# A relative-position bias table moved from the kernel's start to a place between two projection tiles

## The chip, the cores and the metric

One core of a Trainium2 chip runs the whole kernel. The metric is the device time of one execution in microseconds; several executions are timed, and their median counts. All data are float32.

## What is computed

One decoder layer is applied to a prompt group (1 x 1024 tokens) and a sample group (8 x 8 tokens, with key and value caches of 2048 rows) by the same weights: RMSNorm with adaLN shift and scale, one input projection `h @ w_in` to queries, keys, values and a pooling input, attention in three dilated windows, causal pooling, an output projection, and a channel sub-layer of width 4096. What matters here is the bias of the attention. Each branch adds, by head, a bias that depends on the distance between query and key alone:

```python
bias = rel_bias[rel_bucket(jnp.clip(dist, 0, n_sub) * dil)]
logits = logits + jnp.transpose(bias, (2, 0, 1)).astype(jnp.float32)
logits = jnp.where(valid[None, :, None, None], logits, NEG_INF)
...
o, lse over the branches (128, 1), (512, 4), (2048, 16), merged by their softmax denominators
```

The kernel merges the three branches into one softmax. For each of the 8 heads it needs a table over distance: `rel_bias` of the bucket of a distance plus the log of the number of branches that hold that distance (or -1e30 where none does).

## The kernel before

**The order of the work.** The kernel is written in program order and a planner orders the instructions of each engine: an instruction comes when its inputs and buffers are there by the planner's own times, the earlier one in the program first. Buffers come in kinds ("tags") with a fixed number each: "nat" 17 (rows of all 1088 tokens), "raw" 4 (weights as loaded), "wf" 6 (weights split), "tmp" 2, and in PSUM "ps" 8 banks. `tc.issue_after(ins)` keeps the instructions of a block behind `ins` on its engine. On the chip each engine and each DMA queue then runs its list in that order and waits where it must. DMAs issued by `nc.sync` go through SP's queue, those issued by `G.dma_start` through GpSimd's.

**Start (lines 68 to 236).** SP loads the constants `cpk`, eight tiles `x` of 128 x 1088, then the bias tables (below), then the ada weights `wa` (eight tiles of 512 KB for one half, L93 to L97), `us`, and the first two projection weights win4 and win5. ScalarE squares the x tiles into `xsq` (x0 into `acc`), VectorE adds them to `acc` (L195), TensorE sums `acc` over partitions (L205, names `n1`), VectorE and ScalarE make the inverse root `rstd1` of it by a logarithm, an exponential and three Newton ops per half (`newton`, L132 to L135, 512 and 576 wide). Meanwhile TensorE multiplies the ada weights (L101, `pa`); the result is transposed (L110) and added to its bias (L115).

**The bias tables (L175 to L184, L217 to L228, L301 to L312).** `rel_bias` (32 x 8) and the table `onehot` (32 buckets x 3752 distances) come through SP's queue, the latter in four pieces of 1024 columns (`oh`); `logmult` comes as four pieces of 8 rows into `lm`, at partitions 0, 32, 64 and 96. TensorE multiplies each piece in two halves of 512 columns (L224, `pg`, all with `rbias` on partitions 0 to 31), ScalarE copies the eight results to `fb` (L228), and GpSimd adds `fb` to `lm` (L302). Then a copy that needs the last projection input (`mark`, L304) holds back five DMAs from GpSimd's queue: `lm` is written to DRAM, 16 times over, as `gscr` (L309), and its far part as `fscr` (L312). From there the attention reads its bias tiles: `bs` and `bnew` on GpSimd's queue (L386 to L394), `fs` on SP's (`load_bias`, L461).

**Projection inputs and tiles (L258 to L376).** `h1_half` makes, for four x tiles at a time, `hp` on VectorE (L264), its rounded part `h1h` on ScalarE (L265) and the rest `h1l` on VectorE (L279). `gemm` multiplies split weights with split inputs in three passes (L243, L245, L247) into three banks of PSUM per tile. The weights are split by ScalarE (L146) and by VectorE, or for win4 and win5 by GpSimd (L147). Key tiles are 4 to 7, query tiles 0 to 3. `in_tile` also runs two or three steps of the later ada products behind each tile. `QK.tile` copies a result to `nat` (L339) and squares it (L340); `stats` (L351 to L353) and `scale` (L361 to L363, names `kss`, `krb`, `krst`, `qrb`) normalise the keys:

```python
kg, qg = QK(4, gk, "k"), QK(0, gq, "q")
for r in range(4):
    kg.tile(r)
kg.stats()
qg.tile(0)
kg.scale()
```

Behind these stages follow the pooling and value tiles, the attention (an order written out by hand), the output projection and the channel sub-layer.

Of the kernel before, what the change touches and what calls it, by code (L numbers as in the profile page):

```python
# [11 lines left out]
F32 = mybir.dt.float32  # L12
# [5 lines left out]
P = 128  # L18
D = 1024
KD = D // P  # L20
# [5 lines left out]
H = 8  # L26
# [12 lines left out]
GLEN = 2312  # L39
FLEN = 15 * 96  # L40
GREP = 16
# [4 lines left out]
CTX = 15  # L46
# [3 lines left out]
def body(ctx: ExitStack, tc: tile.TileContext, i, o):  # L50
    nc = tc.nc
    mm = nc.tensor.matmul
    V = nc.vector
    S = nc.scalar
    G = nc.gpsimd

    def f(ap):
        return ap.bitcast(F32)

    const = ctx.enter_context(tc.tile_pool(name="const", bufs=1))  # L60
    pools = {"": tc.alloc_tile_pool(name="psum1", bufs=8, space=PSUM)}
    wpool = ctx.enter_context(tc.tile_pool(name="wpool", bufs=3))

    def ps(name, tag="ps"):
        return pools[""].tile([P, 512], F32, tag=tag, name=name, bufs=PSB[tag])
# [5 lines left out]
    def part(name):  # L71
        c0, shape = CPK[name]
        n = math.prod(shape)
        v = cpk[:, c0:c0 + n]
        if len(shape) == 2:
            v = v.rearrange("p (a b) -> p a b", b=shape[1])
        return v

    cT, bT, g1T, g2T, qkg, ident, ones, sel, selb, pscT, rcnt = (part(n) for n in CPK)
    gq = const.tile([P, 1], F32, tag="gq", name="gq")  # L80
    V.tensor_scalar_mul(gq, qkg[:, 0:1], E ** -0.5)
    gk = qkg[:, 1:2]
# [10 lines left out]
    def ada_load(r, hf, k, pool, tag, bufs):  # L93
        t = pool.tile([P, 2, 512], F32, tag=tag, name=f"wa{r}_{hf}_{k}", bufs=bufs)
        src = i["w_ada"][k * P:(k + 1) * P, r * 2048:(r + 1) * 2048].rearrange("p (s c) -> p s c", s=2)
        nc.sync.dma_start(t, src[:, :, hf * 512:(hf + 1) * 512])
        return t  # L97

    def ada_mm(pa, k, t):
        for g in range(4):  # L100
            ins = mm(pa[32 * g:32 * g + 32, :256], cs[:, k, :], t[:, g // 2, (g % 2) * 256:(g % 2 + 1) * 256],  # L101
                     start=(k == 0), stop=(k == KD - 1))
        return ins

    def ada_end(r, hf, pa):
        sb = (wpool if r else nat_pool).tile([P, 256], F32, tag="tmp" if r else "nat", name=f"adas{r}_{hf}", bufs=2 if r else NNAT)
        act = S.copy(sb, pa[:, :256])
        pt = ps(f"pat{r}_{hf}")
        for j in range(2):
            nc.tensor.transpose(pt[:, j * P:(j + 1) * P], sb[:, j * P:(j + 1) * P], ident)  # L110
        for j in range(2):
            src = pt[:, j * P:(j + 1) * P].rearrange("p (s q c) -> p s q c", s=2, c=32)[:, :, :, 0:9]
            idx = aT[:, r * 16:(r + 1) * 16, :].rearrange("p (s h q j) c -> p s h q j c", s=2, h=2, q=2)
            bb = bT[:, r * 16:(r + 1) * 16].rearrange("p (s h q j) -> p s h q j", s=2, h=2, q=2)[:, :, hf, :, j]
            V.tensor_tensor(idx[:, :, hf, :, j, :], src, bb.unsqueeze(3).to_broadcast([P, 2, 2, 9]), ALU.add)  # L115
        return act
# [43 lines left out]
    nat_pool = tc.alloc_tile_pool(name="nat", bufs=NNAT, side="left")  # L160
# [11 lines left out]

    gscr = tc.dram_tile([H, GREP, GLEN], F32, name="gscr")
    fscr = tc.dram_tile([H, FLEN], F32, name="fscr")
    rbias = const.tile([32, H], F32, tag="rbias", name="rbias")  # L175
    nc.sync.dma_start(rbias, i["rel_bias"])
    lm = nat_pool.tile([P, 1024], F32, tag="nat", name="lm")
    G0 = [(32 * n, c0, min(1024, GLEN + FLEN - c0)) for n, c0 in enumerate(range(0, GLEN + FLEN, 1024))]
    ohs = []
    for r0, c0, n in G0:  # L180
        oh = wpool.tile([32, 1024], F32, tag="wf", name=f"oh{c0}", bufs=NWF)
        nc.sync.dma_start(oh[:, :n], i["onehot"][:, c0:c0 + n])
        nc.sync.dma_start(lm[r0:r0 + H, :n], i["logmult"][:, c0:c0 + n])
        ohs.append(oh)  # L184
    wa0 = {(0, k): ada_load(0, 0, k, *(((wpool, "raw", NRAW), (nat_pool, "nat", NNAT))[k // 4])) for k in range(KD)}

    xs = nat_pool.tile([P, KD, NB, TS], F32, tag="nat", name="xs")
# [1 line left out]
    for k in range(KD):  # L189
        if k == 0:  # L190
            S.activation(acc, xts[0], AF.Square)
        else:
            sq = wpool.tile([P, T], F32, tag="tmp", name=f"xsq{k}", bufs=2)
            act = S.activation(sq, xts[k], AF.Square)
# [3 lines left out]
    def rstd_of(acc, rstd, chunks, name):  # L198

        a0, a1 = chunks[0][0], chunks[-1][0] + chunks[-1][1]  # L200
        vv = wpool.tile([P, T], F32, tag="tmp", name=f"{name}v", bufs=2)
        tv = wpool.tile([P, T], F32, tag="tmp", name=f"{name}t", bufs=2)
        for ci, (c0, n) in enumerate(chunks):
            pp = ps(f"{name}_{ci}")
            ins = mm(pp[:, :n], ones, acc[:, c0:c0 + n], start=True, stop=True)  # L205
            V.tensor_scalar(vv[:, c0:c0 + n], pp[:, :n], 1.0 / D, EPS, ALU.mult, ALU.add)
        half = [slice(a0, a0 + 512), slice(a0 + 512, a1)] if a1 - a0 > 600 else [slice(a0, a1)]
        for c in half:
            ln = S.activation(tv[:, c], vv[:, c], AF.Ln)
        with tc.issue_after(ln.ins):  # L210
            for c in half:
                S.activation(rstd[:, c], tv[:, c], AF.Exp, scale=-0.5)
        for c in half:
            newton(rstd[:, c], vv[:, c], tv[:, c])
        return ins

    fb = wpool.tile([P, 1024], F32, tag="wf", name="fb", bufs=NWF)  # L217
    pgs = []
    for d0 in (0, 512):
        pg = ps(f"pg{d0}")  # L220
        for (r0, c0, n), oh in zip(G0, ohs):
            if n > d0:
                w = min(512, n - d0)
                pe = mm(pg[r0:r0 + H, :w], rbias, oh[:, d0:d0 + w], start=True, stop=True)  # L224
                pgs.append((pg, slice(r0, r0 + H), d0, w))
    with tc.issue_after(act.ins):
        for pg, r, d0, w in pgs:
            S.copy(fb[r, d0:d0 + w], pg[r, :w])  # L228
    pa = ps("pa0_0")
    with tc.issue_after(pe.ins):  # L230
        pe = ada_mm(pa, 0, wa0[0, 0])
    with tc.issue_after(pe.ins):
        pe = rstd_of(acc, rstd1, CHUNKS, "n1")
    with tc.issue_after(pe.ins):
        for k in range(1, KD):
            pe = ada_mm(pa, k, wa0[0, k])
# [16 lines left out]
    h1h, h1l = [], []  # L253
# [35 lines left out]
    act = ada_end(0, 0, pa)  # L289
# [3 lines left out]
    pa = ps("pa0_1")  # L293
# [4 lines left out]
            ada_mm(pa, k, wa0[1, k])  # L298
    ada_end(0, 1, pa)
    h1_half(1)  # L300
    for r0, c0, n in G0:  # L301
        G.tensor_add(lm[r0:r0 + H, :n], lm[r0:r0 + H, :n], fb[r0:r0 + H, :n])  # L302
    mark = const.tile([P, 1], F32, tag="mark", name="mark")
    ins = G.tensor_copy(mark, f(h1l[KD - 1][:, 0:1]))  # L304
    with tc.issue_after(ins.ins):
        for r0, c0, n in G0:
            ng = max(0, min(n, GLEN - c0))
            if ng:
                G.dma_start(gscr[:, :, c0:c0 + ng], lm[r0:r0 + H, :ng].unsqueeze(1).to_broadcast([H, GREP, ng]))  # L309
            if ng < n:  # L310
                f0 = c0 + ng - GLEN
                G.dma_start(fscr[:, f0:f0 + n - ng], lm[r0:r0 + H, ng:n])  # L312

    later_ada = ada_steps()

    def in_tile(m):
# [11 lines left out]
    class QK:  # L328
# [26 lines left out]
        def scale(self):  # L355

            for c0, n in CHUNKS:
# [4 lines left out]
                for r in range(4):  # L362
                    V.scalar_tensor_tensor(self.raws[r][:, c], self.raws[r][:, c], self.gvec, rbs[r][:, :n], ALU.mult, ALU.mult)  # L363

    kg, qg = QK(4, gk, "k"), QK(0, gq, "q")
    kT, qT = kg.raws, qg.raws
    for r in range(4):
        kg.tile(r)
    kg.stats()
    qg.tile(0)  # L370
    kg.scale()
# [11 lines left out]
    for hp in range(HP):  # L383
        r0 = 32 * hp
# [128 lines left out]
    for hp in range(HP):  # L513
        for a in range(2):
            r0 = a * E
# [448 lines left out]

CPK, NCPK = {}, 0
for _n, _s in (("cT", (KD, 9)), ("bT", (48,)), ("g1T", (KD,)), ("g2T", (KD,)), ("qkg", (2,)), ("ident", (P,)),
               ("ones", (P,)), ("sel", (32,)), ("selb", (P,)), ("pscT", (4,)), ("rcnt", (4, CTX))):
    CPK[_n] = (NCPK, _s)
    NCPK += math.prod(_s)

# [5 lines left out]
NWF = 6  # L976
# [6 lines left out]
def _distance_tables():  # L983


    far = WB + 7 - np.arange(15)[:, None] - 16 * np.arange(96)[None]
    dist = np.concatenate([GOFF - np.arange(GLEN), far.ravel()])
    d = np.maximum(dist, 1).astype(np.float32)
    large = 16 + (np.log(d / np.float32(16)) / np.float32(math.log(2048 / 16)) * np.float32(16)).astype(np.int32)
    bucket = np.where(dist < 16, dist, np.minimum(large, 31))  # L990
    onehot = ((bucket[None, :] == np.arange(32)[:, None]) & (dist >= 0)[None]).astype(np.float32)
    n = sum(((dist >= 0) & (dist <= w) & (dist % s == 0)).astype(np.int64) for w, s in ((128, 1), (512, 4), (2048, 16)))
    logm = np.where(n > 0, np.log(np.maximum(n, 1)), BIG).astype(np.float32)
    return onehot, np.ascontiguousarray(np.broadcast_to(logm, (H, GLEN + FLEN)))


def _tiles(w, m):
# [91 lines left out]
```

## Time and profile before

| What | Value |
|---|---|
| Median of 3 runs | 1374.87 us (1372.66 to 1382.95) |
| The profiled execution, its own time | 1385.76 us |
| Its span, first to last instruction | 1384.0 us |
| Mean granted TensorE clock | 0.978 |
| Busy: TensorE (PE) | 1325.9 us, 96% |
| Busy: VectorE (DVE), ScalarE (ACT), GpSimd (POOL) | 584.5, 390.1, 119.0 us |

The profile is one execution taken by the hardware profiler. Times are microseconds from the span's start, durations in some views are nanoseconds. PE is the matmul side of TensorE, PEld its weight loads, SPq and POOLq the DMA queues of SP and GpSimd. L302 is line 302 of the kernel. A granted clock of 1.00 is 2.4 GHz, of 0.50 is 1.2 GHz. In brackets behind a row stands how long its engine was idle before it and what it waited for.

### The profile page before, as it was taken

How to read it: one execution, taken by the hardware profiler on the slowest of the kernel's cores; microseconds unless marked ns; L12 is line 12 of the kernel's file. 1: busy time of each engine (PE TensorE's matmuls, PEld its weight loads, DVE VectorE, ACT ScalarE, POOL GpSimd, SP SyncE). 2: the span in 40 equal slices, each digit the busy share in tenths (PEclk: the TensorE clock that was granted, in tenths of full speed). 3: DMA queues.
4: the chain of work that ended last, by engine and by line, in shares of the span. 5: the costliest groups of instructions: out<-in, count | busy, mean ns of one | idle time of the engine just before them, and what ended most of it. 6: DMA issues, size and time to landing. Idle time of an engine off the chain costs nothing.

```text
span 1384.0 us, 21247 instructions
## 1 busy us (share of the span) xinstructions
PE 1325.9 (96%) x9060; PEld 1112.8 (80%) x9060; DVE 584.5 (42%) x1120; ACT 390.1 (28%) x660; POOL 119.0 (9%) x175
## 2 busy tenths in 40 slices
PE   3698999998999999999999999999999999999998
PEld 1485777894665567999999999999999999999998
DVE  5643233314656565577332433432433324334333
ACT  6232030224766653435202202112012012021120
POOL 3201002611212000000000000000000000000000
PEclk9899799998999999999999999999999999999999
DMA  9686433427767563482961541721814615411002
GB/s 322 209 112 170 133 124 125 157 93 287 249 208 268 174 232 113 133 282 70 338 207 46 186 149 47 260 74 45 274 46 133 201 46 186 149 47 46 31 33 97
DMA packets 48719, 211.09 MB, mean 153 GB/s; under 512 B 6432, under 2 KB 6688, under 8 KB 47600
## 3 DMA queue, kind: packets, MB, share of 16 engines
q1 hardware_dynamic: 44752, 137.17, 30.3%
q0 software_dynamic: 3872, 72.56, 16.6%
q8 instruction: 71, 1.16, 0.3%
q14 instruction: 24, 0.20, 0.0%
HBM read 199.28 MB, written 77.27 MB: 200 GB/s over the span
## 4 chain that ended last, share of the span: by engine, by line
PE 90%; DMA 4%; DVE 3%; ACT 2%; issue 1%; SPq 0%; DVEq 0%; ACTq 0%
PE dn L245 9%; PE dn L243 9%; PE dn L247 9%; PE up L245 9%; PE up L247 9%; PE up L243 9%; PE z L243 5%; PE z L247 5%; PE z L245 4%; PE po L715 2%; PE pt L705 2%; PE S L660 2%; PE spo L618 1%; PE pa L101 1%; PE sl L572 1%; PE ob L247 1%
## 5 line engine op out<-in xcount | busy, mean ns | idle before, releaser
L831 DVE SCALAR_TENSOR_TENSOR X<-dn,aT,X 128x512 f32<-128x512 f32 (+2 forms) x192 | 98.4, 568 | 204.5 <-PE dn L247 204.5
L863 POOL COPY mark<-fh 128x1 f32<-128x1 f32 x7 | 8.5, 1218 | 561.9 <-ACT fh L930 561.9
L931 DVE TENSOR_TENSOR fl<-r,fh 128x1088 fp32r<-128x1088 f32 x32 | 41.3, 1292 | 35.5 <-ACT fh L930 35.5
L528 ACT ACTIVATE L<-L,m 128x128 f32<-128x128 f32 (+7 forms) x64 | 49.1, 770 | 19.2 <-DVE m L532 19.2
L708 ACT COPY PT<-pt 128x512 f32<-128x512 f32 (+1 forms) x80 | 41.7, 541 | 39.2 <-PE pt L705 30.4
L705 PE MATMUL pt<-cpk,L 128*128 128x128 f32 x288 | 45.4, 284 | 2.6 <-ACT PT L708 1.5
L930 ACT CAST fh<-r 128x1088 fp32r<-128x1088 f32 x32 | 35.4, 1105 | 44.1 <-DVE r L927 44.1
L705 PEld LDWEIGHTS pt<-cpk,L 128*128 128x128 f32 x288 | 31.2, 141 | 18.0 <-issue 10.9
L245 PE MATMUL dn<-fh,wd_3l 128*128 128x288 f32 (+1 forms) x192 | 43.4, 328 | 0.0
L243 PE MATMUL dn<-fh,wd_3h 128*128 128x288 f32 (+1 forms) x192 | 43.4, 328 | 0.0
L247 PE MATMUL dn<-fl,wd_3h 128*128 128x288 f32 (+1 forms) x192 | 43.4, 328 | 0.0
L243 PE MATMUL dn<-fh,wd_1h 128*128 128x288 f32 (+1 forms) x192 | 42.5, 328 | 0.0
L245 PE MATMUL dn<-fh,wd_1l 128*128 128x288 f32 (+1 forms) x192 | 42.5, 328 | 0.0
L247 PE MATMUL dn<-fl,wd_1h 128*128 128x288 f32 (+1 forms) x192 | 42.3, 328 | 0.0
L245 PE MATMUL dn<-fh,wd_0l 128*128 128x288 f32 (+1 forms) x192 | 42.3, 328 | 0.0
L243 PE MATMUL dn<-fh,wd_0h 128*128 128x288 f32 (+1 forms) x192 | 42.2, 328 | 0.0
L245 PE MATMUL dn<-fh,wd_2l 128*128 128x288 f32 (+1 forms) x192 | 42.2, 328 | 0.0
L243 PE MATMUL dn<-fh,wd_2h 128*128 128x288 f32 (+1 forms) x192 | 42.2, 328 | 0.0
L247 PE MATMUL dn<-fl,wd_2h 128*128 128x288 f32 (+1 forms) x192 | 42.2, 328 | 0.0
L247 PE MATMUL dn<-fl,wd_0h 128*128 128x288 f32 (+1 forms) x192 | 42.1, 328 | 0.0
L927 DVE TENSOR_TENSOR r<-r 128x1088 f32<-128x1088 f32 x32 | 41.1, 1286 | 0.0
L532 DVE CUSTOM_DVE_ANT_0 L<-S,fs 128x384 f32<-128x384 f32 (+5 forms) x64 | 32.0, 538 | 18.7 <-PE S L660 18.5
(942 smaller groups left out, 3393.2 us busy)
## 6 DMA issues: line engine op xcount, KB each, us to landing
out_kw<-in_cache_k POOLq DMA_DIRECT2D x8, 4080.0 KB, 15.8
out_vw<-in_cache_v POOLq DMA_DIRECT2D x8, 4080.0 KB, 29.2
wa<-in_w_ada SPq DMA_DIRECT2D x48, 512.0 KB, 4.7
kc<-in_kc SPq DMA_DIRECT2D x40, 512.0 KB, 5.1
vc<-in_vc SPq DMA_DIRECT2D x40, 512.0 KB, 4.9
x<-in_xT SPq DMA_DIRECT2D x8, 544.0 KB, 8.5
X<-in_xT SPq DMA_DIRECT2D x8, 544.0 KB, 7.5
fs<-gscr SPq DMA_DIRECT2D x8, 512.0 KB, 7.7
```

The source lines that it names most:

```text
L243: mm(pt[:, :n], wh[:, kw], xh(k, c0, n), start=st, stop=False)
L245: mm(pt[:, :n], wl[:, kw], xh(k, c0, n), start=False, stop=False)
L247: mm(pt[:, :n], wh[:, kw], xl(k, c0, n), start=False, stop=sp)
L528: last["act"] = S.activation(L[:, :n], L[:, :n], AF.Exp, bias=negm, scale=-1.0, accum_out=sm)
L532: V.tensor_tensor_reduce(out=L[:, c0:c0 + n], in0=pt, in1=bias, scale=-1.0, scalar=(3.0e38 if prev is None else prev), op0=ALU.add, op1=AL ...
L660: mm(pts[a][:, :nm], w[r, qc], m[r, c0:c0 + nm], start=(x == 0), stop=(x == 2))
L705: nc.tensor.transpose(pt[:, n * P:(n + 1) * P], u["L"][:, a, ii * nk0 + j * P:ii * nk0 + (j + 1) * P], ident)
L708: later(0, lambda: S.copy(PT[:, :n * P], pt[:, :n * P]))
L831: V.scalar_tensor_tensor(X[:, m, c0:c0 + npr], pt[:, :npr], aT[:, base + m, 0:1], X[:, m, c0:c0 + npr], ALU.mult, ALU.add)
L927: V.tensor_tensor(r, r, r, ALU.mult)
L930: S.copy(fh, r)
L931: V.tensor_sub(fl, r, f(fh))
```

## The change

The tables no longer come at the start. `rel_bias` is repeated on the host for four groups of 32 partitions and becomes a part of the constants `cpk`; `onehot` and `logmult` are laid out on the host as 128 x 1024, one group of 32 partitions for each 1024 distances. A function `bias_table` loads both through GpSimd's queue into two nat tiles, multiplies each group by its own copy of `rel_bias`, adds the result to `lm` on VectorE straight from PSUM, and issues the five writes to `gscr` and `fscr` with no mark ahead of them. It is called behind the second key tile. The copies to `fb` on ScalarE, the adds on GpSimd and the `issue_after` blocks around them are gone.

```diff
-    cT, bT, g1T, g2T, qkg, ident, ones, sel, selb, pscT, rcnt = (part(n) for n in CPK)
+    cT, bT, g1T, g2T, qkg, ident, ones, sel, selb, pscT, rcnt, rbias = (part(n) for n in CPK)
...
-    rbias = const.tile([32, H], F32, tag="rbias", name="rbias")
-    nc.sync.dma_start(rbias, i["rel_bias"])
-    lm = nat_pool.tile([P, 1024], F32, tag="nat", name="lm")
-    G0 = [(32 * n, c0, min(1024, GLEN + FLEN - c0)) for n, c0 in enumerate(range(0, GLEN + FLEN, 1024))]
-    ohs = []
-    for r0, c0, n in G0:
-        oh = wpool.tile([32, 1024], F32, tag="wf", name=f"oh{c0}", bufs=NWF)
-        nc.sync.dma_start(oh[:, :n], i["onehot"][:, c0:c0 + n])
-        nc.sync.dma_start(lm[r0:r0 + H, :n], i["logmult"][:, c0:c0 + n])
-        ohs.append(oh)
...
-    fb = wpool.tile([P, 1024], F32, tag="wf", name="fb", bufs=NWF)
-    pgs = []
-    for d0 in (0, 512):
-        pg = ps(f"pg{d0}")
-        for (r0, c0, n), oh in zip(G0, ohs):
-            if n > d0:
-                w = min(512, n - d0)
-                pe = mm(pg[r0:r0 + H, :w], rbias, oh[:, d0:d0 + w], start=True, stop=True)
-                pgs.append((pg, slice(r0, r0 + H), d0, w))
-    with tc.issue_after(act.ins):
-        for pg, r, d0, w in pgs:
-            S.copy(fb[r, d0:d0 + w], pg[r, :w])
     pa = ps("pa0_0")
-    with tc.issue_after(pe.ins):
-        pe = ada_mm(pa, 0, wa0[0, 0])
+    pe = ada_mm(pa, 0, wa0[0, 0])
...
-    for r0, c0, n in G0:
-        G.tensor_add(lm[r0:r0 + H, :n], lm[r0:r0 + H, :n], fb[r0:r0 + H, :n])
-    mark = const.tile([P, 1], F32, tag="mark", name="mark")
-    ins = G.tensor_copy(mark, f(h1l[KD - 1][:, 0:1]))
-    with tc.issue_after(ins.ins):
-        for r0, c0, n in G0:
...
+    mark = const.tile([P, 1], F32, tag="mark", name="mark")
+
+    def bias_table():
+
+        oh, lm = [nat_pool.tile([P, 1024], F32, tag="nat", name=n) for n in ("oh", "lm")]
+        G.dma_start(oh, i["onehot"])
+        G.dma_start(lm, i["logmult"])
+        for d0 in (0, 512):
+            pg = ps(f"pg{d0}")
+            for r0 in range(0, P, 32):
+                mm(pg[r0:r0 + 32, :], rbias[r0:r0 + 32, :], oh[r0:r0 + 32, d0:d0 + 512], start=True, stop=True)
+            V.tensor_add(lm[:, d0:d0 + 512], lm[:, d0:d0 + 512], pg)
+        for n in range(4):
+            r, c0 = slice(32 * n, 32 * n + H), 1024 * n
+            w = min(1024, GLEN + FLEN - c0)
+            ng = max(0, min(w, GLEN - c0))
+            if ng:
+                G.dma_start(gscr[:, :, c0:c0 + ng], lm[r, :ng].unsqueeze(1).to_broadcast([H, GREP, ng]))
+            if ng < w:
+                f0 = c0 + ng - GLEN
+                G.dma_start(fscr[:, f0:f0 + w - ng], lm[r, ng:w])
+
     kg, qg = QK(4, gk, "k"), QK(0, gq, "q")
     kT, qT = kg.raws, qg.raws
     for r in range(4):
         kg.tile(r)
+        if r == 1:
+            bias_table()
...
-    return onehot, np.ascontiguousarray(np.broadcast_to(logm, (H, GLEN + FLEN)))
+    pad = ((0, 0), (0, 4096 - GLEN - FLEN))
+    onehot = np.pad(onehot, pad).reshape(32, 4, 1024).transpose(1, 0, 2).reshape(P, 1024)
+    return onehot, np.repeat(np.pad(logm[None], pad).reshape(4, 1024), 32, 0)
...
+        "rbias": np.tile(np.pad(np.asarray(rel_bias), ((0, 0), (0, 32 - H))), (4, 1)),
```

## Rows read from the trace of the kernel before

**Rows 1.** The page's slices: the granted TensorE clock in 40 equal slices of the span, in tenths of full speed.
```profile
PEclk9899799998999999999999999999999999999999
```
**Rows 2.** The chain of work that ended last, in order of time, in the first 110 us: start, length, what.
```profile
7.53 10.36 DMA oh<-in_onehot
18.03 4.36 PE pg L224 x14
...
40.16 1.28 DVE hp L264
```
**Rows 3.** The timeline of SP's queue: start and length of the issue, line, what is loaded.
```profile
17.51 0.31 SPq L182 DMA_DIRECT2D oh<-in_onehot  x1
...
18.23 4.12 SPq L96 DMA_DIRECT2D wa<-in_w_ada  x8
22.39 0.55 SPq L397 DMA_DIRECT2D us<-in_stT  x1
...
24.95 0.38 SPq L96 DMA_DIRECT2D wa<-in_w_ada  x1
```
**Rows 4.** Stages: the window and its length, busy time (and instructions) of PE, PEld, DVE, ACT and POOL, the granted clock, the DMA engines' busy share, GB/s.
```profile
14.50:19.00 4.50, 0.97 (x4) 0.44 (x7) 4.19 (x4) 3.67 (x4) 1.04 (x2) 1.00 0.60 108
19.00:43.00 24.00, 12.43 (x89) 4.84 (x83) 16.00 (x18) 10.98 (x17) 12.80 (x6) 0.79 1.03 376
...
78.00:104.00 26.00, 26.00 (x159) 23.30 (x158) 6.73 (x12) 5.66 (x11) 3.20 (x6) 1.00 0.82 64
```
**Rows 5.** VectorE's instructions by form in 25 to 43 us (busy us, mean ns of one, idle before), and two rows of GpSimd's timeline.
```profile
L133 DVE SCALAR_TENSOR_TENSOR n1t<-rstd 128x576 f32<-128x576 f32 x1 | 2.9, 2902 | 0.0
L135 DVE SCALAR_TENSOR_TENSOR rstd<-n1t,rstd 128x512 f32<-128x512 f32 x1 | 2.8, 2821 | 0.0
...
L134 DVE TENSOR_TENSOR n1t<-n1t,n1v 128x512 f32<-128x512 f32 x1 | 2.1, 2107 | 0.0
...
L133 DVE SCALAR_TENSOR_TENSOR n1t<-rstd 128x512 f32<-128x512 f32 x1 | 0.7, 692 | 2.7 <-ACT rstd L212 2.7
...
25.39 9.67 POOL L302 TENSOR_TENSOR lm<-lm,fb 8x1024 f32<-8x1024 f32 x4 [7.45 <-ACT fb L228]
...
35.63 2.85 POOL L147 TENSOR_TENSOR win4l<-win4r,win4h 128x1024 fp32r<-128x1024 f32 x1
```
**Rows 6.** Timelines of the start: GpSimd's copies, each started by the landing of an x tile; the squares of x2 and then x0 in ScalarE's order; VectorE's seven adds to `acc`; TensorE's column sums and the last ada step of the first half.
```profile
8.92 0.23 POOL L196 COPY xs<-x 128x64 f32<-128x64 f32 x1 [1.11 <-DMA x<-in_xT]
...
14.40 0.75 POOL L196 COPY xs<-x 128x64 f32<-128x64 f32 x1 [0.65 <-DMA x<-in_xT]
17.54 0.40 POOL L196 COPY xs<-x 128x64 f32<-128x64 f32 x1 [2.40 <-DMA x<-in_xT]
...
8.89 1.11 ACT L194 ACTIVATE xsq<-x 128x1088 f32<-128x1088 f32 x1 [0.24 <-DMA x<-in_xT]
9.90 1.09 ACT L191 ACTIVATE acc<-x 128x1088 f32<-128x1088 f32 x1
...
11.03 9.60 DVE L195 TENSOR_TENSOR acc<-acc,xsq 128x1088 f32<-128x1088 f32 x7 [7.04 <-ACT acc L191]
...
23.38 3.49 PE L205 MATMUL n<-acc,cpk 128*128 128x512 f32 x6
...
31.73 0.64 PE L101 MATMUL pa<-wa,cs 128*32 128x256 f32 x8 [0.70 <-DMA wa<-in_w_ada]
```
**Rows 7.** The timeline of TensorE: the first matmul of z6 and two later ones (only z6 stands between these two), and an ada step.
```profile
70.31 0.55 PE L243 MATMUL z<-h1h,win6h 128*128 128x512 f32 x1 [2.16 <-ACT win6h L146]
...
76.31 0.50 PE L245 MATMUL z<-h1h,win6l 128*128 128x512 f32 x1
...
80.14 0.53 PE L247 MATMUL z<-h1l,win4h 128*128 128x512 f32 x2
...
126.50 0.64 PE L101 MATMUL pa<-wa,cs 128*32 128x256 f32 x8
```
**Rows 8.** GpSimd's timeline around the writes of the table (the second row is the first read that waits for them), and in the chain the piece with which z5 ends.
```profile
78.39 2.02 POOL L309 DMA_DIRECT2D gscr<-lm  x3
...
105.07 0.59 POOL L389 DMA_DIRECT2D bs<-gscr  x1 [23.60 <-DMA gscr<-lm]
...
87.54 0.72 PE z L247 x4
```
**Rows 9.** From the landing of the table to the first matmul of query tile 1: SP's timeline, the chain (start, length, what), a stage as in rows 4, and TensorE's timeline of the keys' and then the queries' scaling with the first matmul behind each.
```profile
104.44 0.63 SPq L461 DMA_DIRECT2D fs<-gscr  x1
...
110.32 12.19 DMA win1r<-in_w_in
...
123.61 1.23 DVE win1l L147
...
148.00:152.00 4.00, 4.00 (x14) 3.58 (x14) 0.00 (x0) 0.00 (x0) 0.53 (x1) 0.50 0.93 332
...
132.89 2.08 PE L361 MATMUL krb<-krst,cpk 32*128 32x512 f32 x6 [4.38 <-DVE krst L135]
...
146.94 1.04 PE L243 MATMUL z<-h1h,win1h 128*128 128x512 f32 x2
...
206.75 1.14 PE L361 MATMUL qrb<-qrst,cpk 32*128 32x512 f32 x8
...
215.17 0.80 PE L243 MATMUL z<-h1h,win13h 128*128 128x512 f32 x1
```

More of the change, by code (lines that the diff above doesn't have):

```diff
@@ L300, in body @@
     h1_half(1)
-    for r0, c0, n in G0:
-        G.tensor_add(lm[r0:r0 + H, :n], lm[r0:r0 + H, :n], fb[r0:r0 + H, :n])
-    mark = const.tile([P, 1], F32, tag="mark", name="mark")
-    ins = G.tensor_copy(mark, f(h1l[KD - 1][:, 0:1]))
-    with tc.issue_after(ins.ins):
-        for r0, c0, n in G0:
[L307 to L312, printed above, removed]
     later_ada = ada_steps()
@@ L966 @@
 for _n, _s in (("cT", (KD, 9)), ("bT", (48,)), ("g1T", (KD,)), ("g2T", (KD,)), ("qkg", (2,)), ("ident", (P,)),
-               ("ones", (P,)), ("sel", (32,)), ("selb", (P,)), ("pscT", (4,)), ("rcnt", (4, CTX))):
+               ("ones", (P,)), ("sel", (32,)), ("selb", (P,)), ("pscT", (4,)), ("rcnt", (4, CTX)), ("rbias", (32,))):
     CPK[_n] = (NCPK, _s)
@@ L1039 @@
         "w_ada": np.asarray(w_ada)[0],
-        "rel_bias": np.asarray(rel_bias),
         "onehot": onehot,
```

## The prediction

> **What bounds the kernel now.** Read the busy shares and the granted clock first: TensorE (PE) is busy 96% of the span, and nearly all slices in which it runs below full speed lie at the beginning [rows 1]. So a microsecond is won or lost for good where PE waits in the first 150 us; behind that, whatever PE gained stays gained. The second view is the chain that ended last, followed from the start: it does not run through the activations or the weights but through the bias. From the onehot tables' landing (17.9 us) it goes to the bias matmuls pg, to the ScalarE copies of pg into fb, and only then to the statistics of the first norm, its Newton steps on VectorE and the first projection input at 40.16 us [rows 2]. Third, SP's queue: it issues small table loads between the x tiles and the weights, each only when an earlier transfer has landed, so the first ada weight leaves at 18.23 us [rows 3]; the stage table shows the DMA engines 60% busy at 108 GB/s in 14.5 to 19 us, against 103% and 376 GB/s right after [rows 4]. Fourth, VectorE by form in 25 to 43 us: a 512-wide op takes 0.69 us or 2.1 to 2.8 us, the long ones while GpSimd works [rows 5].
>
> **What the change takes out of the start.** Nine loads leave SP's queue, the 16 pg matmul records leave PE, the fb copies leave ScalarE, the four 8-row adds leave GpSimd.
> (1) The norm's column sums. They start at 23.38, behind pg and one ada step; what they need is acc, whose seven adds start at 11.03 and last 9.60, so 20.63 [rows 6]. I keep that start of the adds, because ScalarE's order is the planner's and I see no reason why it changes. The matmul could start at 20.7: 2.7 us earlier. If ScalarE squared x0 first, the last x tile would decide: x tiles land every 1.37 us (8.92 to 14.40 is four of them) and the eighth, delayed by the tables to 17.54, would land near 15.8; one square (1.1) and one add (1.4) later is 18.3, another 2.4 us.
> (2) Newton. While GpSimd's 9.67 us of lm adds ran, the 576-wide op took 2.90 where 0.69 x 576/512 = 0.78 was due, and a 512-wide one 2.11 instead of 0.69; that is 2.1 + 1.4 = 3.5 us. The third long one (2.82 instead of 0.69) stands beside the split of win4 (L147), which stays; it keeps its 2.1 us [rows 5].
> What is late next? The ada product needs its eighth weight, landed at 31.73; with SP feeding only large loads, eight tiles of 0.52 MB at 376 GB/s behind 15.8 give 27, some 5 us sooner, and win4, next in the queue, shifts by as much [rows 4, 6]. Both lie before the first projection input's new time, 40.2 - 6.2 = 34 [rows 2]. So the start gains 2.7 + 3.5 = 6.2 us; bounds 3.5 (half of (1) lost to PE's order, and a longer hold by win4) and 8.8.
>
> **What it adds.** Two table loads of 512 KB on GpSimd's queue, 8 matmuls (16 records), two adds of 128x512 on VectorE, the same five writes to gscr and fscr.
> Where do they run? The tables are tiles of the pool "nat", 17 buffers. SP took us, far down in the program, before the ada weight that is first of its half; that weight lies in nat too, and at that moment 16 nat tiles at the most were given out (eight x, lm, four weights, xs, acc, rstd1), so nothing but its turn held it: buffers of one kind are given in program order [rows 3]. ScalarE's order says the same: x0 is squared after x1 and x2, since acc's turn in nat comes late [rows 6]. So the tables wait for k1 and its squares, and the block runs about where it is written, behind the second key tile.
> (3) PE. Eight records of 256 columns of the ada product, four at a time in the same way, take 0.64 us at full clock [rows 7]; pg has twice the records and twice the columns, 2.6 us, and 0.4 for the turn of operands: 3.0 us on PE, which is full there (26.00 of 26 us [rows 4]). Nothing hides it. Bounds: 0, if the planner puts it into a hole such as the 2.16 us of [rows 7], and 4.4, what the old pg took [rows 2]; if the table is not there in time, its landing is added: 1.05 MB at 376 GB/s are 2.8 us [rows 4], with issue and latency 5 at the most, my ceiling.
> (4) PSUM. pg takes its two banks before z6, so z6 can no longer fill holes before z5 is done. It did: its first piece waited 2.16 us for win6h with PE idle [rows 7]. That wait goes, and the later pieces of z4 and z5 can take the places of z6's. I take 1 us gained, between -1 and 2.2.
> The adds on VectorE (some 0.7 us each, as the 512-wide op [rows 5]) lie beside 26 us in which it works 6.7 [rows 4]: nothing.
> (5) What the writes hold up. From the first issue at 78.39 to the read that waits for them at 105.07 it is 26.7 us, and beside them the DMA engines are 82% busy at 64 GB/s [rows 4, 8]. SP's queue stands at the read fs, which waits for them until 104.44, and the weights queued behind it come all at once: win1 leaves at 110.32 and needs 12.2 us to land. VectorE has win1's split ahead of the last key statistic, so krst is late, and PE stands still from 128.5 to 132.89, falls, after that idling, to a granted clock of 0.50 (1.2 of 2.4 GHz) and stays there until 152 [rows 9]. Now the writes start later in the program: not after h1 but after z5, the loads, pg and the adds. The planner sees that too, and the two weights that then have free buffers, and win1 itself if the ada steps fill PE's wait for the table, go into SP's queue ahead of fs. Then krst is ready when z0 ends. Worth: the idle 4.4 us; at the most also the slow clock. The query tiles' same step at the better clock took 206.75 to 215.17, 8.4 us, the keys' 132.89 to 146.94, 14.0: 5.6 more, and 2.5 of the 5 us to 152 [rows 9]. Bounds: 12.5 gained, or by rival C the lead lost. I take 5, the idle time and little of the clock.
>
> **A rule that speaks against GpSimd's queue.** Here the first three writes from that queue took 2.02 us to issue [rows 8]; none was held. The Trainium skill, "SBUF — State Buffer", section "SBUF: two separate sides", says that descriptors of a DMA issued from GpSimd can't be written while VectorE runs an op that holds the shared port pair, about 620 ns becoming 3100. By that (an estimate) the two table loads would leave 5 us later; the sum doesn't need it, since the 5 us for a late table are already a bound of (3).
>
> **Sum.** -6.2 + 3.0 - 1.0 - 5 = -9.2 us. The profiled execution took 1385.76 (span 1384.0 and 1.8 around it), 0.8% above the median 1374.87; all terms are waits and work of the first 150 us, so they carry over in microseconds: 1376.6 on its scale, 1365.7 on the runs'. Bounds: -8.8 + 0 - 2.2 - 12.5 = -23.5 and with C's 9.2 for the other end.
>
> **Rivals.**
> B: only the start is won. win1 stays behind fs and lands as late relative to PE as now. For it: win1 left 6 us after fs did, so something besides fs, a buffer most likely, held it too [rows 9]. Then (5) is 0: -4.2, 1370.7.
> C, the other side: fs stays ahead of the weights as in SP's present order [rows 3, 9], and the end of the writes sets z1. Now z1 follows the landing by 42.5 us (104.44 to 146.94). Whatever the start won is then waited away, and the total moves with the landing alone. It decides at one point: lm complete before or after 78.4 us. z5 ends today near 88.2 (87.54 + 0.72), with z6 alone on PE from 76.3 to 80.1 ahead of it [rows 7, 8]; less 6.2 and those 3.8 it ends at 78.2 at the earliest, so the pg and the adds (3.0 + 1.4) complete lm at 82.6, 4.2 us later than today's 78.4, and a late table adds up to 5. The landing, and with it z1, comes 4.2 to 9.2 us later: 1379, to 1384.
> D: the tables do not wait for a turn, GpSimd loads them at once into free nat buffers, pg runs in the first 15 us and the writes fall into the stream of 19 to 43 us, which has no room (103% busy [rows 4]). 1 MB more costs 2.8 us at 376 GB/s, 24 us of writes up to 20, against 6.2 won and, of the later wait, some 8: +8, 1383. Against it: the order of us and acc above.
>
> **How the numbers follow.** Sum as argued: 0.50, its own range 1357 to 1371. B 0.22, C 0.18, D 0.10. The range 1353 to 1383 holds the gains' far end but for a tenth, and B and most of C; D and the late table of C lie at its upper edge. A measurement of this kernel tells about 1% from no change (13.7 us): faster than 1361.1 needs the clock part of (5), about half of the first case and a little of B: 0.28. Slower than 1388.6 needs D or C with something added: 0.10. Within 1%: 0.62.
>
> **What would show it.** (1), (2): n1's first matmul near 20.7, no 512- or 576-wide op over 1 us before win4's split, the first projection input near 34 instead of 40.16. No table load in SP's queue, and DMA engines full from 5 to 40 us. (3): pg of about 2.6 us on PE between z5 and z6, with no wait for oh. (5): win1's issue before fs in SP's queue, no idle PE at krb, and 1.00 clock there. I am wrong if the gscr writes are issued before 50 us, if win1 still leaves after the landing of gscr, or if the lead at z4 is not there any more at z1.

## Result, and the profile after

The changed kernel takes 1365.62 us (median of 6 runs, 1363.17 to 1367.14) against 1374.62 for the kernel before beside it: ratio 0.9915, 95% interval 0.989 to 0.994. Measured again (e9 below): 1367.49, ratio 0.9931 (0.9906 to 0.9957). So it is faster by some 9 us, under 1%, where 9.2 were forecast. The profiled execution took 1366.97 (span 1365.2).

The two profiles differ by 18.8 us and the medians by 9.0, so the profile of before was of one of its longer executions. A second one (e1) stands beside it; starts on TensorE (PE) in us (here and below, a tile "ends" where its last matmul starts):

| | before, profiled (1385.76) | before, e1 (1372.09) | changed (1366.97) | changed, e9 (1369.28) |
|---|---|---|---|---|
| z4 starts | 42.7 | 43.1 | 36.8 | 37.0 |
| z7 ends | 108.5 | 108.9 | 107.4 | 106.5 |
| z0 starts | 111.5 | 111.9 | 109.5 | 108.7 |
| krb starts | 132.9 | 128.9 | 126.1 | 125.3 |
| z1 starts | 146.9 | 138.5 | 132.8 | 133.8 |
| last dn ends | 1379.9 | 1366.2 | 1361.0 | 1363.3 |

Six us are won at z4, of which one to two are left at z7 and two to three at z0. The rest comes between z0 and z1: 10 to 12 us against the profile of before, 1.5 to 3.3 against e1.

The start. First the stages of the changed kernel that answer to [rows 4] (columns as there), then PE's and VectorE's timelines (start, length, line, what, idle before), against [rows 2, 5, 6].
```profile
14.50:19.00 4.50, 1.08 (x8) 0.23 (x8) 4.19 (x4) 3.55 (x4) 1.34 (x2) 1.00 1.04 389
19.00:43.00 24.00, 14.14 (x91) 8.33 (x95) 18.20 (x22) 9.65 (x15) 6.58 (x4) 0.79 0.85 314
78.00:104.00 26.00, 26.00 (x161) 22.03 (x160) 8.76 (x14) 6.56 (x12) 2.88 (x5) 1.00 0.80 100
```
```profile
20.57 3.99 PE L195 MATMUL n<-acc,cpk 128*128 128x512 f32 x6 [2.45 <-DVE acc L185]
...
36.78 1.03 PE L220 MATMUL z<-h1h,win4h 128*128 128x512 f32 x2 [7.61 <-ACT h1h L242]
```
```profile
27.75 1.36 DVE L133 SCALAR_TENSOR_TENSOR n1t<-rstd 128x512 f32<-128x512 f32 x2 [2.69 <-ACT rstd L202]
29.02 1.35 DVE L134 TENSOR_TENSOR n1t<-n1t,n1v 128x512 f32<-128x512 f32 x2
30.29 3.50 DVE L135 SCALAR_TENSOR_TENSOR rstd<-n1t,rstd 128x512 f32<-128x512 f32 x2
...
34.26 1.28 DVE L241 SCALAR_TENSOR_TENSOR hp<-x,A,rstd 128x1024 f32<-128x1024 f32 x1
```
The DMA engines are full from the first weight on (389 GB/s where 108 had been; in 19 to 43 us their share is 1.03 to 1.05 up to 37 us and 0.28 behind that), the column sums wait for acc alone, and only the third pair of Newton steps is long, beside the split of win4 on GpSimd.

The table: GpSimd's loads and writes, and the product on PE, against [rows 8].
```profile
42.91 0.72 POOL L334 DMA_DIRECT2D oh<-in_onehot  x1 [1.74 <-DVE hp L241]
45.77 0.55 POOL L335 DMA_DIRECT2D lm<-in_logmult  x1 [2.14 <-DVE hp L241]
85.86 1.84 POOL L346 DMA_DIRECT2D gscr<-lm  x3 [39.54 <-DVE lm L340]
...
108.95 0.59 POOL L377 DMA_DIRECT2D bs<-gscr  x1 [20.21 <-DMA gscr<-lm]
```
```profile
81.24 1.92 PE L339 MATMUL pg<-oh,cpk 32*32 32x512 f32 x16
```
The loads wait for VectorE to be done with an x tile (their buffers' turn, not the queue), and the product waits for nothing. The table leaves 7.5 us later than before and lands 3.9 later.

From z7 to z1: SP's queue, ScalarE, PE, the stages at krb (columns as in [rows 4]) and the page's clock row, against [rows 1, 9].
```profile
74.82 8.09 SPq L96 DMA_DIRECT2D wa<-in_w_ada  x3
85.00 0.34 SPq L152 DMA_DIRECT2D win1r<-in_w_in  x1
108.33 1.25 SPq L449 DMA_DIRECT2D fs<-gscr  x2
```
```profile
95.02 1.05 ACT L146 CAST win1h<-win1r 128x1024 fp32r<-128x1024 f32 x1 [10.67 <-PE z L222]
...
117.47 1.11 ACT L140 ACTIVATE krst<-ktv 128x1088 f32<-128x1088 f32 x1
```
```profile
126.11 1.13 PE L325 MATMUL krb<-krst,cpk 32*128 32x512 f32 x6
...
132.79 0.50 PE L220 MATMUL z<-h1h,win1h 128*128 128x512 f32 x1
```
```profile
125.00:130.00 5.00, 5.00 (x50) 1.65 (x48) 3.37 (x9) 0.94 (x3) 0.00 (x0) 1.00 0.75 252
130.00:135.00 5.00, 4.15 (x23) 1.86 (x22) 2.71 (x5) 1.04 (x1) 0.00 (x0) 1.00 0.44 170
```
```profile
PEclk9899989999999999999999999999999999999999
```
win1 leaves 25 us earlier than in [rows 9], ahead of fs. Its cast on ScalarE is done at 96, krst follows the key statistics at once, krb has no idle time before it, and the clock, 0.50 in [rows 9], is 1.00 there. The 7 that [rows 1] have in the fifth slice (138 to 173 us) is gone.

### The profile page after: what moved, and what is told of

Same layout as the page of the kernel before. It is cut to its first block, busy times and chain, and to the rows that moved or that the text cites. A ratio compares the mean times of both kernels' runs of the same rounds, so it can differ in the third digit from the quotient of the medians.

```text
span 1365.2 us, 21230 instructions
## 1 busy us (share of the span) xinstructions
PE 1312.7 (96%) x9060; PEld 1108.2 (81%) x9060; DVE 581.8 (43%) x1122; ACT 385.8 (28%) x652; POOL 111.0 (8%) x172
## 4 chain that ended last, share of the span: by engine, by line
PE 92%; DVE 3%; DMA 3%; ACT 2%; issue 1%; SPq 0%; DVEq 0%; ACTq 0%
PE dn L222 9%; PE dn L220 9%; PE dn L224 9%; PE up L222 9%; PE up L220 9%; PE up L224 9%; PE z L220 5%; PE z L224 5%; PE z L222 5%; PE po L703 2%; PE pt L693 2%; PE S L648 2%; PE spo L606 2%; PE sl L560 1%; PE ob L222 1%; PE ob L224 1%
## 5 line engine op out<-in xcount | busy, mean ns | idle before, releaser
L919 DVE TENSOR_TENSOR fl<-r,fh 128x1088 fp32r<-128x1088 f32 x32 | 41.3, 1292 | 35.4 <-ACT fh L918 35.4
L516 ACT ACTIVATE L<-L,m 128x128 f32<-128x128 f32 (+7 forms) x64 | 49.1, 769 | 18.5 <-DVE m L520 18.5
L101 PE MATMUL pa<-wa,cs 128*32 128x256 f32 x384 | 29.0, 399 | 21.5 <-DMA wa<-in_w_ada 21.5
L222 PE MATMUL dn<-fh,wd_2l 128*128 128x288 f32 (+1 forms) x192 | 42.2, 328 | 0.0
L220 PE MATMUL dn<-fh,wd_2h 128*128 128x288 f32 (+1 forms) x192 | 42.2, 328 | 0.0
L224 PE MATMUL dn<-fl,wd_2h 128*128 128x288 f32 (+1 forms) x192 | 42.2, 328 | 0.0
```

What stands on the lines that cost most here:

```text
L220: mm(pt[:, :n], wh[:, kw], xh(k, c0, n), start=st, stop=False)
L222: mm(pt[:, :n], wl[:, kw], xh(k, c0, n), start=False, stop=False)
L224: mm(pt[:, :n], wh[:, kw], xl(k, c0, n), start=False, stop=sp)
L516: last["act"] = S.activation(L[:, :n], L[:, :n], AF.Exp, bias=negm, scale=-1.0, accum_out=sm)
L919: V.tensor_sub(fl, r, f(fh))
```

## The experiments

Theory as predicted: SP's order (fs ahead of win1 or behind) decides what happens at krb, and the start's gain goes through to z1. Rivals: B, something else holds win1; C, the landing of gscr sets z1. All ratios are against the kernel before on the same chip; its medians on the three chips used for e1 to e4, e5 to e8 and e9 to e12 are 1376.31, 1374.97 and 1377.78 us, so differences in us across these groups carry some 3 us. A, B and C are the three ada weights that stand ahead of win1 in SP's queue.

**e1, the kernel before again.** 

> The kernel before, unchanged, for a second profile and for the clock of every run. Its profiled execution took 1385.76 us and its runs lie in two groups (near 1373 to 1375 and near 1382 to 1386). Theory: the stretch of low granted TensorE clock at krb (rows 9) is there only in the executions of the upper group, so a profile of 1373 to 1375 us shows clock 1.00 from 132 to 152 us, and z1 starts some 8 to 10 us earlier than 146.94. Rival: the stretch is there in every execution, and the two groups differ elsewhere; then z1 starts at 147 again and the clock falls there again. Ratio to before 1.000 by both.

1376.00 us, ratio 0.9983 (0.9958 to 1.0009), profile of an execution of 1372.09. SP, ScalarE and PE:
```profile
101.64 0.63 SPq L461 DMA_DIRECT2D fs<-gscr  x1
...
110.66 0.34 SPq L152 DMA_DIRECT2D win1r<-in_w_in  x1
```
```profile
118.55 1.05 ACT L146 CAST win1h<-win1r 128x1024 fp32r<-128x1024 f32 x1 [7.31 <-DMA win1r<-in_w_in]
```
```profile
128.92 1.13 PE L361 MATMUL krb<-krst,cpk 32*128 32x512 f32 x6
```
The theory held but for the end of the stretch. gscr landed 2.8 us earlier here, fs left earlier, and win1 took 7.9 us to its cast instead of the 12.2 of [rows 9]. krst came in time, krb's first matmul did not wait, the clock was 1.00 in 130 to 135 us and 0.97 in 135 to 140 (0.69 in 140 to 145), and z1 started 8.4 us earlier. A table that lands 2.8 us earlier goes with an execution shorter by 13.7; these are two executions, and that fs beside win1 is what slowed its load is not shown. In three sets of runs of the kernel before 15 of 35, 11 of 29 and 21 of 35 lay above 1377 us. Of the changed kernel's 18 runs none lay above 1370.4.

**e2, fs behind win1 in the kernel before.**
```
+        with tc.issue_after(loads["win1"].ins):
             nc.sync.dma_start(fs, ...)
```


> The kernel before with the scatter of the bias table (fs) held behind win1's load on SP's queue: the tables themselves stay where they were, so this is term (5) alone. Theory (the order on SP's queue pays): A, B, C and win1 land before fs, krb does not wait, -5 to -12.5 us, the lower end if the execution of before has no low clock at krb. Rival B (only the start is won): 0, within 1 us. Rival C (fs late makes z1 wait for the scatter): slower, +4 to +9.

1374.58, ratio 0.9979 (0.9957 to 1.0000). SP, and the row of all ada steps on PE from 58 to 119 us (count, durations in ns, first to last start):
```profile
89.63 22.39 SPq L96 DMA_DIRECT2D wa<-in_w_ada  x3
112.12 0.41 SPq L154 DMA_DIRECT2D win1r<-in_w_in  x1
113.05 1.25 SPq L464 DMA_DIRECT2D fs<-gscr  x2
```
```profile
L101 PE MATMUL pa<-wa,cs x96: 379/379/404, 58.6 to 111.7; 128*32 128x256 f32 x96
```
My theory's price falls. With fs out of the way win1 still left at 112.12: the ada weights ahead of it wait for a buffer, and the last ada step that frees it stands on PE behind z7 (111.7). With fs behind it, win1 took 6.0 us to its cast instead of 12.2, and the runs reach only to 1378.4; the interval of the ratio touches 1.

**e5, no product** (the bias values are left out: oh is added in the product's place).
```
-            pg = ps(f"pg{d0}")
-            for r0 in range(0, P, 32):
-                mm(pg[r0:r0 + 32, :], rbias[...], oh[...], start=True, stop=True)
...
+        V.tensor_add(lm[:, 0:512], lm[:, 0:512], oh[:, 0:512])
...
```


> The changed kernel without the one-hot product: oh's own tile is added where the product was, and sixteen matmuls and their PSUM tile are gone (the bias is left out so). By the product's own length on PE (81.24 to 83.16): -2 us against the changed kernel, 1363.6 us. If the product also costs what terms (3) and (4) together were short by (z6 can start only behind it): -4 to -5, 1361 us. If the end is set by loads from 85 us on: 0, 1365.6.

1379.29, ratio 1.0017 (0.9993 to 1.0041): slower than the changed kernel by 12 to 14 us, which none of the three expected. z7 ends at 103.8, 2.7 to 3.6 us ahead of the changed kernel (106.5 in e9, 107.4). But the planner, with the product gone, puts the last ada steps behind z7. The same row for e5, then for the changed kernel, and what follows in e5 on SP, ScalarE and PE, with a stage:
```profile
L101 PE MATMUL pa<-wa,cs x64: 379/379/636, 57.9 to 104.7; 128*32 128x256 f32 x64
```
```profile
L101 PE MATMUL pa<-wa,cs x64: 379/379/493, 57.9 to 76.7; 128*32 128x256 f32 x64
```
```profile
109.55 1.25 SPq L446 DMA_DIRECT2D fs<-gscr  x2
110.90 0.54 SPq L96 DMA_DIRECT2D wa<-in_w_ada  x1
111.53 0.42 SPq L152 DMA_DIRECT2D win1r<-in_w_in  x1
```
```profile
121.93 1.05 ACT L146 CAST win1h<-win1r 128x1024 fp32r<-128x1024 f32 x1 [15.73 <-DMA win1r<-in_w_in]
```
```profile
131.94 2.08 PE L325 MATMUL krb<-krst,cpk 32*128 32x512 f32 x6 [8.24 <-DVE krst L135]
```
```profile
135.00:140.00 5.00, 5.00 (x26) 1.36 (x22) 4.01 (x7) 0.00 (x0) 0.00 (x0) 0.50 0.33 105
```
This is the new theory: the last ada step of that half, which frees a buffer, decides when win1 can leave. In four kernels win1 leaves 0.4 to 0.9 us behind it: 93.1 and 93.6 (e6), 103.4 and 103.8 (e7), 109.4 and 110.3 (before), 111.7 and 112.1 (e2). In the changed kernel it is 76.7 and 85.0: there the step is out of the way, and win1 waits until VectorE's split of win0 (83.76 to 84.97) has freed a buffer. In e5 it is 104.7 and 111.5: the last ada weight and win1 stand behind fs in SP's queue, and fs waits for gscr until 109.55, as the prediction had it.

**e3, the additions of lm later in the kernel before.**
```
+    m0 = G.tensor_copy(mark0, f(h1l[3][:, 0:1]))
+    with tc.issue_after(m0.ins):
         ... G.tensor_add(lm, lm, fb)
```


> The kernel before with the two additions of lm on GpSimd held until the fourth tile of h1: term (2) alone, without the column sums that start earlier. Theory: n1's Newton steps are no longer held by the additions, hp starts 3.5 us earlier (36.7 for 40.16), and SP's queue is as before, so -3.5 us, of which at krb's wait a part may be given back: -1 to -3.5. Rival (what the start wins is waited for at krb, whose weights come no earlier): 0.

1380.17, ratio 1.0018 (0.9993 to 1.0042). PE:
```profile
38.19 1.03 PE L243 MATMUL z<-h1h,win4h 128*128 128x512 f32 x2 [3.70 <-ACT h1h L265]
44.34 1.03 PE L247 MATMUL z<-h1l,win4h 128*128 128x512 f32 x2 [4.07 <-DVE h1l L279]
```
The rival's number was right, not its place: z4 starts 4.9 us earlier than in e1, but the lead is lost long before krb, since PE stands for h1l: VectorE's next two ops (2.59 and 3.37 us) now lie beside GpSimd's splits of win4 and win5, and the additions (51.45 to 60.5) beside later ones. z7 ends at 109.0 as in e1 (108.9). Here an overlap with GpSimd that was only moved won nothing.

**e8, the tables' loads on SP's queue** instead of GpSimd's.
```
-        G.dma_start(oh, i["onehot"])
+        nc.sync.dma_start(oh, i["onehot"])
```


> The changed kernel with oh's and lm's loads issued on SP's queue instead of GpSimd's, behind A, B, C and ahead of win1. If the queue alone matters: the product at 81 us waits for oh, which is issued only near 75 to 77 us, +0 to +3 us, 1365.6 to 1369. If the loads' place in the program is what frees SP's queue at the start, and not the queue: 0, 1365.6 within 1.5 us. If SP's queue is held at the start as before, the first weights come late again: +6, 1371.6.

1373.71, ratio 1.0000 (0.9981 to 1.0019): 6 us above e9.
```profile
87.16 3.63 PE L339 MATMUL pg<-oh,cpk 32*32 32x512 f32 x16 [7.15 <-DMA oh<-in_onehot]
```
SP reached oh only at 81.66, behind three ada weights whose issue, with waits for buffers, took 8.09 us. The first sort of expectation had the place right and the price too low; the third had the price by another way, for z4 starts at 36.9 here as in the changed kernel. The Trainium skill, "DMA: Bandwidth & Descriptors", section "Issuing engines are not separate DMA queues", says that issuing from several engines saves only the usually small time of the issue; here the second queue was worth 7.15 us on PE, since a load is not queued behind others that wait.

**e4, fs ahead of A, B, C and win1 in the changed kernel** (load_bias(0) and (1) called behind bias_table; the four loads held behind them).
```
+        with tc.issue_after(held["fs"].ins) if name == "win1" else ExitStack():
             nc.sync.dma_start(raw, src)
...
```


> The changed kernel with fs issued on SP's queue right behind the table's way out to memory, and the ada weights A, B, C and win1 held behind it (rival C's order, term (5) undone). Theory (the order on SP's queue pays): krb waits for win1, z1 starts some 42 us behind the landing of gscr, +5 to +18 us against the changed kernel, 1371 to 1384 us, that is 0.997 to 1.007 of the kernel before. Rival (the place of fs is of no account): 1365.6 us as the changed kernel, 0.9935.

1385.95, ratio 1.0052 (1.0027 to 1.0076): 18 to 20 us above the changed kernel, beyond the upper end. ScalarE and PE:
```profile
126.28 1.04 ACT L149 CAST win1h<-win1r 128x1024 fp32r<-128x1024 f32 x1 [29.73 <-DMA win1r<-in_w_in]
```
```profile
129.86 1.92 PE L319 MATMUL kss<-ksq,cpk 128*32 128x512 f32 x2 [18.50 <-ACT ksq L308]
```
ScalarE has win1's cast ahead of the last squares of the keys, as in the changed kernel; with win1 landing at 126 that cast held squares, statistics and PE. z1 starts at 152.3, 42.2 us behind the landing of gscr, as expected; PE's wait is not at krb but ahead of it.

**e10 and e11, win1's split behind krst**, in the kernel before and in e4.
```
+        with tc.issue_after(exps[0].ins) if name == "win1" else ExitStack():
             S.copy(hi, raw)
             eng.tensor_sub(lo, raw, f(hi))
```


> The kernel before with one thing changed: win1's split (its cast on ScalarE and its subtraction on VectorE) is issued behind the exponential that makes krst. Nothing of the bias table is touched. Theory (what costs time at krb is that krst's two activations stand behind win1's cast on ScalarE, and the cast waits for a load that is issued behind fs): krst is ready near 119 us, krb starts at once behind pa near 127 to 128 in every execution, the clock stays at 1.00, z1 starts near 134 to 135, and the runs form one group near 1367 to 1370, ratio 0.993 to 0.997. Rival (krb's wait comes from the weights that pa reads, which land as late): krb's wait moves to pa, two groups as before, ratio 1.000.

> The kernel of e4_fs_first (the changed kernel with fs ahead of A, B, C and win1) with win1's split issued behind krst's exponential as in e10_split_late. Theory (the place of fs on SP's queue costs time only through win1's cast on ScalarE): the 18.5 us that PE stood at ksq are gone, krb waits for nothing but A, B and C, z1 waits for win1 until some 129, and the time is near the changed kernel's, 1366 to 1370, against 1386 in e4_fs_first. Rival (the late loads themselves hold PE, whatever ScalarE's order): 1378 or more.

e10: 1373.26, ratio 0.9979 (0.9954 to 1.0004); krb at 128.1 without a wait for krst, clock 1.00 until 135, z1 at 137.4, 10 of 12 runs below 1375 (6 of 12 in e1); the interval of the ratio holds 1. e11: 1376.23, 9.7 below e4, still 8.7 above e9. Both were to come out lower. e11 on VectorE and PE:
```profile
128.08 1.23 DVE L153 TENSOR_TENSOR win1l<-win1r,win1h 128x1024 fp32r<-128x1024 f32 x1 [8.57 <-ACT win1h L152]
```
```profile
131.98 2.08 PE L332 MATMUL krb<-krst,cpk 32*128 32x512 f32 x6 [6.20 <-DVE krst L138]
```
ScalarE's order was half of it. VectorE has win1's subtraction between krst's Newton steps, and it stood 8.57 us there. The Trainium skill, "PSUM — Partial Sum Buffer", section "Engine vs sequencer instructions", calls the queues of both strict FIFO; these rows agree.

**e6 and e7, the table behind the third and the fourth key tile** (`if r == 2`, `if r == 3`).

> The changed kernel with the call that makes the table behind the third tile of the key projection instead of the second: z6's pieces can again fill PE's waits in z4 and z5. If the loss of these pieces is what terms (3) and (4) were short by: -2 to -4 us, 1361.5 to 1363.5. If the table is then late for z1 (gscr written some 12 us later, 98 for 85.86, and fs behind it), slower by up to 8: to 1373. If neither: 1365.6.

> The changed kernel with the call behind the fourth tile of the key projection. The start is as in the changed kernel, the table leaves some 24 us later. By the theory that the table was early enough (its use in z1 lies at 132 us and later): -2 to -4 us, 1361.5 to 1363.5. If fs, which then lands some 24 us later, comes too late for z1: slower by 10 to 20, 1375 to 1385.

e6: 1370.03, ratio 0.9967 (0.9945 to 0.9990). z6 starts at 65.9 again instead of 83.1 and z7 still ends at 107.4: filling holes with z6 gains nothing. fs leaves 10 us later (118.12) and with it the two ada weights behind it (124.88). win2 leaves when it does in the changed kernel (126.30, 126.28), but lands in 7.7 us instead of 5.7; VectorE has its split ahead of the rest of the keys' scaling, and PE waits 2.00 us for that. z2 starts 1.9 to 3.3 us later than in the changed kernel's two profiles. e7: 1392.91, ratio 1.0130 (1.0100 to 1.0160); fs leaves at 136.85, and PE's waits are those of rival C, on ada weights queued behind fs (total, times, longest in us):
```profile
PE pa L101 <- DMA wa<-in_w_ada: 26.0, 3, 21.9
```

**e9 and e12, the changed kernel again, and with the product in the second half of z4 and z5** (table written out where it is now, fs behind win1, win1's split behind krst).

> The changed kernel itself, beside the next three on one chip. Its six runs lay between 1363.17 and 1367.14 us. Theory (its krb never waits for win1, so no execution has the low clock at krb): again one narrow group, all within 6 us, median 1364 to 1368, ratio to before 0.990 to 0.995. Rival (the runs of the kernel before fall in two groups for a reason outside the kernel): here too a second group some 8 us above the first.

> The changed kernel with the product ahead of the key projection's second half (PE waits there for weights), its way out to memory held until the second key tile's copy as now, fs held behind win1's load, and win1's split behind krst's exponential. e5_no_product ended z7 at 103.8 us and the changed kernel at 107.4, so the product costs 3.6 us where it stands. Theory (PE's waits for weights between 50 and 72 us can take the product in): z7 ends near 104 to 105, -2 to -3.5 us against the changed kernel, 1362 to 1364. Rival (the waits there move with the product, as the pieces of z4 and z5 come later too): z7 ends at 107 again, 1365.6; if oh lands late for the new place: +1 to +3.

e9: the 12 runs lie within 8 us (6 had been expected), one group. e12: 1367.87, ratio 0.9933 (0.9908 to 0.9957), the same time as e9, and z7 ends at 106.5 in both. PE in e12:
```profile
61.01 1.04 PE L225 MATMUL z<-h1h,win4h 128*128 128x512 f32 x2 [3.12 <-ACT h1h L247]
...
63.98 3.16 PE L344 MATMUL pg<-oh,cpk 32*32 32x512 f32 x16
```
The rival was right: PE waits for h1h instead, the ada steps come later, the last at 107.4, and nothing of the product's price is won. e12 shows one thing more: win1 leaves as late as in the kernel before (111.61, 110.32) and its cast is at 120.1, yet krb does not wait for krst, since the split stands behind krst's activations. No kernel beat the changed one.

## Why the prediction was right, point by point

(1) and (2) came as worked out: column sums 20.57 (20.7), hp 34.26 (34), z4 5.9 us earlier (6.2), the third Newton pair still long. What was wrong is that this lead counted in full. At z7 it is 1.1 us (2.4 in e9 against e1). (3) The product's own rows are 1.92 us, not 3.0: no run shows the 0.4 for a turn of operands, and sixteen ada records in a row take 1.07 us, not twice 0.64. (4) gained nothing: PE's wait for win6h is gone as forecast (2.2 us before), but behind 60 us PE now waits 4.5 us (3.2 in e9) for the weights of ada steps that stand earlier, 1.4 before and 1.7 in e5. From z4's start to z7's end it is 65.8 us before and in e1, 66.3 in e5, and 70.6 and 69.5 changed: 3.2 to 4.3 against the 2.0 of (3) and (4). About 1.1 us of this is not lost: 14 ada records that before and e5 have behind z7 (1.06 us in e6, where they stand in one row) now run ahead of it. Lead at z0: 4.2 forecast, 2.0 to 3.2 measured.

(5) named the right place and the right effect, idle time and clock at krb, and mis-sized them. From z0 to z1 it is 35.4 us before, 26.6 in e1, and 23.3 and 25.1 changed: between 1.5 and 12.1 gained. With 9.0 and 10.3 between the medians and 2.0 to 3.2 of lead, some 6 to 8 on average (an estimate: what is left of the medians), where I took 5. The cause as I put it, writes that hold SP at fs, is not the whole: in [rows 9] win1 was held until 110.32 by the buffer that the last ada step frees (e2), as rival B said. B was wrong that the change leaves this as it is: with the product where it stands, the planner puts those steps ahead of z6 (e5 undoes it). The prediction had this only as a condition, "if the ada steps fill PE's wait for the table".

What joins the runs is when win1's cast comes. Here are the cast and the last Newton step of krst in before, then that step in e1 and in the changed kernel:
```profile
122.52 1.05 ACT L146 CAST win1h<-win1r 128x1024 fp32r<-128x1024 f32 x1 [11.63 <-DMA win1r<-in_w_in]
...
131.46 1.29 DVE L135 SCALAR_TENSOR_TENSOR krst<-ktv,krst 128x1088 f32<-128x1088 f32 x1
```
```profile
127.48 1.29 DVE L135 SCALAR_TENSOR_TENSOR krst<-ktv,krst 128x1088 f32<-128x1088 f32 x1
```
```profile
121.27 1.29 DVE L135 SCALAR_TENSOR_TENSOR krst<-ktv,krst 128x1088 f32<-128x1088 f32 x1
```
In the kernel before, krst is ready 10.2 us behind the start of the cast: cast at 122.5 and krst at 132.8 (the profile of before), 121.4 and 131.6 (e3), 118.6 and 128.8 (e1), 118.1 and 128.3 (e2). In the first two PE has nothing left and waits 4.38 and 2.76 us at krb; in the last two krst is there just before PE gets to krb (128.9 and 130.7). A few us in win1's landing decide. In the changed kernel the cast is at 95.0, krst is ready at 122.6, and krb starts at 126.1.

C's mechanism exists: e4 and e7 show it, at 18 to 27 us, more than its 13 to 18. The changed kernel escapes it because the ada weights and win1 have left by 85.0, before fs. D did not happen; GpSimd's loads waited for x buffers as argued. The rule that speaks against GpSimd's queue did not show: the two loads took 0.72 and 0.55 us to issue.

That the sum came out 0.1 us from the median is luck: the lead was 1 to 2 us less than forecast and (5) gave 1 to 3 more. Open is what happens behind z1: the 14.1 us there are 18.8 at the end in the profiled pair, and 4.7 become 2.9 between e1 and e9. Of these changes 2.3 and 2.6 us arise between the first matmul of z12 and the first of the channel sub-layer: 427.6 us in the profile of before, 423.3 in e1, 425.3 and 425.9 in the changed kernel's two. So this stretch moved by 4 us between two executions of one kernel, and "whatever PE gained stays gained" holds only within that.

## What to carry to other kernels

Before pricing a stall by the transfer that a queue stands at, look for the buffer that the next entry needs, and for the instruction that frees it: moving the transfer away (e2) shows which of the two holds. A prefetched operand's split standing in an in-order engine ahead of the work that is due makes a late load stop everything behind it (e4: 18.5 us), so ask of each engine, not of one, what stands behind such a split (e11). And look at several executions before a stretch of slow clock in one profile is priced: in the second profile of before it was short (0.69 in 140 to 145 us).

## What was not expected of the hardware

The same write of the table took 23.5 us in one execution of before and 21.2 in another (median from issue to landing of the two large pieces); with the longer one win1 took 12.2 us to land, with the shorter 7.9 to its cast. PE, after idle times of 4.38, 6.20 and 8.24 us at krb, ran at 0.50 of the clock (1.2 of 2.4 GHz) there. But a shorter stop is not free either: in e9 an ada step between the pieces of krb waits 1.54 us and in e1 the last piece of krb 1.63, and the granted clock is 0.88 and 0.78 in 130 to 140 us (e9), 0.69 in 140 to 145 us (e1); in e12 it is 0.50 in 135 to 140 us behind a stop of 1.58. In e2, behind a stop of 1.38 us, it stayed at 1.00. So part of the 2 us by which e9's profile lies above the first one of the changed kernel may be this.
